# Normalization factors kept as rows in DRAM and applied at the output projection of a hybrid decoder trunk

## The chip, the cores and the metric

The kernel runs on one core of one Trainium2 chip. The metric is the device time of one execution in microseconds. Before the change it is 3005.91 us (median of three runs, 3005.88 to 3008.18). A difference of 0.2% is about 6 us.

## The reference, cut to what matters

A trunk of two layers on a sequence of 1024 tokens and a model width of 1024. Each layer has three head groups that read one normed input, an output projection over their concatenated outputs, and a gated MLP with a convolution. What the change touches is how the three groups are normed before the projection:

```
# recurrent group, width 512, in four blocks of 128
y = gelu(gb) * h
return rmsnorm(y, norm_g)                          # one factor per token over all 512
# differential attention, 4 heads of 128
o = rmsnorm(o, norm_g) * (1.0 - lambda_init)       # one factor per token and head
# mLSTM, 4 heads of 128
h = num / max(|den|, exp(-m))                      # then rmsnorm per token and head,
                                                   # times sigmoid(o_pre)
x = x + concat([recurrent, attention, mlstm]) @ w_out    # 1536 -> 1024
```

So there are nine token factors in a layer: one for the recurrent group, four for the attention heads, four for the mLSTM heads. Each is a vector of 1024 numbers, one per token.

## The kernel before, in words

Activations lie transposed: 128 features on the partitions, 1024 tokens along the free axis, so a block of a head's output is one tile of 128x1024 floats (512 KB). A factor per token is therefore a row that has to stand on all 128 partitions. Matrix products are made of three passes in a rounded format: a high and a low part of both operands, high by high, low by high and high by low (L135 to L137); the parts come from `split`, a cast on ACT (L127) and a subtraction on DVE (L128).

A layer is a mixer (about 0 to 796 us and 1512 to 2296 us) and an MLP (the rest). The mixer's program is a list of steps, ORDER, one list per layer: `R0` to `R3` are the four recurrent blocks, `A0` to `A7` the attention heads in two halves each, `z0` to `z11` the mLSTM's input projections with their convolutions, `M0` to `M7` the mLSTM heads in halves, `y0` to `y2` the loading of four blocks each for the output projection (`y0` recurrent, `y1` attention, `y2` mLSTM) and `w0` to `w5` the projection itself. The steps have priorities in that order, and a scheduler merges them into one fixed instruction list per engine before the program runs. An engine works through its list in order. SP's list is almost only DMA issues, and it too stands still at an issue whose data are not ready.

How a factor comes about: the squares of a block (ACT) are summed over the partitions by `compact`, eight matmuls of one column each, which give a 128x8 tile (token i\*128+p in row p, column i). The inverse root is taken on that small tile on DVE (`rsqrt`, last line L232). Then `bcast_half` turns a half of it into a row on all partitions: four matmuls of 128x128 against an identity into a PSUM bank named `pbc` (L240). DVE multiplies the block with the bank in the same instruction as with the norm's weight (L696 for attention, L891 for the mLSTM), SP stores the block to DRAM (`yd`), and `yload` (L1009) loads it at the projection. For the recurrent group each block's squares have a `compact` of their own (L246, `aux<-ones_d,rg`) and are added up in a small tile, `rgacc`; the row is copied from `pbc` to SBUF by ACT (L996) and multiplied in on DVE at the load (L1011).

SBUF tiles come from pools with few buffers. The pool `mu` has two: the convolution results of the steps `z` live in it until their store to DRAM (`mqk<-mu`, L781) has landed. `yst`, the tile that `yload` loads into, is one of four buffers that it shares with other tiles. Weights come through three buffers, `wraw` (L111), ahead of their use.

Of the kernel before, what the change touches and what calls it, by code (L numbers as in the profile page):

```python
# [17 lines left out]
P = 128  # L18
# [11 lines left out]
D_IN = 2 * RG_W + 3 * DA_W + 4 * ML_W + 8  # L30
D_MIX = 1536
ORDER = (
    "v0 r s0 R0 q0 g q2 q3 q1 A0 z3 z1 v1 A1 z0 A2 R1 z2 A3 A4 A5 M0 M1 z6 A6 A7 z5 z4 z11 M2 z8 R2 M3 R3 z7 z9 z10 y1 M4 y0 M5 w3 M6 s1 w1 M7 w0 w2 y2 w5 w4".split(),
    "R0 q0 q1 g z0 v0 z7 v1 q3 A0 q2 A1 A2 z2 A3 A4 z1 z3 z5 A5 M0 z4 z6 M1 R1 A6 A7 M2 z8 R2 M3 R3 z11 M4 z9 z10 y1 M5 y0 M6 M7 w3 w2 w0 w1 y2 w4 w5".split(),
)
PRI = 4000
FFN_CHUNKS = (8, 6, 8)
# [15 lines left out]
class Trunk:  # L53
# [181 lines left out]
    def bcast_half(self, r, j, ps):  # L235
        nc = self.nc
        pb = ps.tile([P, HALF], F32, tag="aux", name=self.nm("pbc"))
        for i in range(4):
            c = 4 * j + i
            nc.tensor.matmul(pb[:, i * P : (i + 1) * P], r[:, c : c + 1].broadcast_to([P, P]),  # L240
                             self.ident, start=True, stop=True)
        return pb

    def compact(self, pc, sq, ones):
        for i in range(8):
# [221 lines left out]
    def rg(self, l, n):  # L467
        nc, a, d = self.nc, self.a, self.lay[l]
        if n == 0:
            self.rgacc = self.sm("rgacc", (P, 8), bufs=1)  # L470
        for _ in (0,):
            A = self.x16("rg")
            u, r, i, w = (A[:, j, :] for j in range(4))
            self.conv4(l, n * P, d["rcw"], d["rcb"], n, 4, u)
            uh, ul = self.mu("uh", F32R), self.mu("ul", F32R)
            self.split(u, uh, ul)
            self.zfeat(l, RG_W + n * P, lambda z, t: nc.vector.tensor_tensor(w[:, t], z, self.rstd[:, t], ALU.mult))
            nc.scalar.activation(w, w, AF.Gelu_apprx_tanh)
            gh, gl = (self.tp.tile([P, HALF], F32R, tag="qk", bufs=10, name=self.nm("rgw")) for _ in range(2))
            raw = self.tp.tile([P, HALF], F32, tag="st", bufs=2, name=self.nm("rgst"))  # L480
            nc.sync.dma_start(raw[:, :P], a["rg_wa"][l, n])
            nc.sync.dma_start(raw[:, P : 2 * P], a["rg_wx"][l, n])
            self.split(raw[:, : 2 * P], gh[:, : 2 * P], gl[:, : 2 * P])
            for gi, bias, o in ((0, d["ba2"], r), (1, d["bx2"], i)):
                z = self.sc.tile([P, S], F32, tag="sc", name=self.nm("rgz"))
                gs = slice(gi * P, gi * P + P)
                for h in range(2):
                    t = slice(h * HALF, (h + 1) * HALF)
                    self.mm3(z[:, t], [((gh[:, gs], gl[:, gs]), (uh[:, t], ul[:, t]))])
                nc.scalar.activation(o, z, AF.Tanh, bias=bias[:, n : n + 1], scale=0.5)  # L490
            t5 = self.p4("rgt")
            nc.scalar.activation(t5, r, AF.Tanh, bias=d["nls4"][:, n : n + 1], scale=d["nls4"][:, n : n + 1])
            nc.scalar.activation(r, r, AF.Exp, bias=d["ls4"][:, n : n + 1], scale=d["ls4"][:, n : n + 1])
            nc.vector.scalar_tensor_tensor(i, i, 1.0, u, ALU.add, ALU.mult)
            nc.scalar.activation(u, r, AF.Square)
            nc.vector.scalar_tensor_tensor(t5, u, 1.0, t5, ALU.add, ALU.mult)
            nc.scalar.activation(t5, t5, AF.Sqrt, scale=0.25)
            nc.vector.tensor_tensor(i, i, t5, ALU.mult)
            nc.vector.tensor_tensor_scan(u, r, i, 0.0, ALU.mult, ALU.add)
            nc.vector.tensor_tensor(u, u, w, ALU.mult)  # L500
            self.yd[n] = self.dr("yd")
            nc.sync.dma_start(self.yd[n], u)
            nc.scalar.activation(i, u, AF.Square)
            pc = self.aux()
            self.compact(pc, i, self.ones_d)
            if n == 0:
                nc.vector.tensor_copy(self.rgacc, pc[:, :8])
            else:
                nc.vector.tensor_tensor(self.rgacc, self.rgacc, pc[:, :8], ALU.add)
        if n < 3:  # L510
            return
        v = self.sm("nv", (P, 8))
        nc.vector.tensor_scalar(v, self.rgacc, 2.0, EPS, ALU.mult, ALU.add)
        self.rg_r = self.sm("rgr", (P, 8), bufs=1)
        self.rsqrt(self.rg_r, v)

    def da_qk(self, l, h):
        nc = self.nc
# [115 lines left out]
    def da_attn(self, l, h, g):  # L634
# [48 lines left out]
            nc.scalar.copy(o[:, g * HALF : (g + 1) * HALF], acc)  # L683
        if g == 0:
            return
        sq = self.o4("sq")
        nc.scalar.activation(sq, o, AF.Square)
        pc = self.aux()
# [2 lines left out]
        nc.vector.scalar_tensor_tensor(v, ss[:, :, 0], EPS, ss[:, :, 0], ALU.mult, ALU.mult)  # L691
        nc.vector.tensor_tensor(v, v, pc[:, :8], ALU.add)
        self.rsqrt(r, v)
        for j in range(2):
            t = slice(j * HALF, (j + 1) * HALF)
            nc.vector.scalar_tensor_tensor(o[:, t], o[:, t], d["dn2"], self.bcast_half(r, j, self.ps), ALU.mult, ALU.mult)  # L696
        self.yd[4 + h] = self.dr("yd")
        nc.sync.dma_start(self.yd[4 + h], o)

    def ml_rows(self, l):  # L700
        nc, a, d = self.nc, self.a, self.lay[l]
# [117 lines left out]
    def ml_head(self, l, h, hf):  # L819
# [66 lines left out]
        th = self.p4("th")  # L886
        nc.sync.dma_start(th, self.mod[h])
        nc.vector.scalar_tensor_tensor(num, th, 1.0, num, ALU.add, ALU.mult)
        for j in range(2):
            t = slice(j * HALF, (j + 1) * HALF)  # L890
            nc.vector.scalar_tensor_tensor(num[:, t], num[:, t], d["mn2"][:, h : h + 1],  # L891
                                           self.bcast_half(r, j, self.ps), ALU.mult, ALU.mult)
        self.yd[8 + h] = self.dr("yd")
        nc.sync.dma_start(self.yd[8 + h], num)

# [16 lines left out]
    def mixer(self, l):  # L912
        nc = self.nc
        with ExitStack() as c:
            self.zp = self.pool(c, "mz", 2, space=PSUM)
            self.sc = self.pool(c, "msc", 2, space=PSUM)
            self.ps = self.pool(c, "maux", 2, space=PSUM)
            self.tp = self.pool(c, "mt", 2)
            self.yd = [None] * 12
            self.pads = [self.tp.tile([P, S + 3], F32, tag=f"mpad{i}", bufs=1, name=self.nm("mpad"))  # L920
                         for i in range(2)]
            self.npad = 0
            for t in self.pads:
                nc.gpsimd.memset(t[:, 0:3], 0.0)
            if l == 0:
                g0 = self.const.tile([P, 8], F32, name="g0")
                self.rows_to_cols([self.a["attn_norm"][0].rearrange("(n p) -> n p", p=P)], g0)
                self.vw0 = [], []

                def early(k, j):  # L930
                    if j == 0:
                        self.v_weight(0, 2 * RG_W + 2 * DA_W, k, *self.vw0, wide=True)

                self.norm_split(g0, self.ps, lambda j: self.o4("nsq")[:, :HALF], True, True, self.load_x, early)
            else:
                for col in self.first_blocks(ORDER[l]):
                    self.pre[l, col] = self.wblock(self.a["w_in"][l][:, col : col + P], KD)

                def nsq(j):
                    return self.wp.tile([P, HALF], F32, tag="wraw", bufs=3, name=self.nm("nsq"))  # L940

                self.norm_split(self.lay[l]["an"], self.ps, nsq, True, True)
            self.qd, self.kd, self.mqd, self.mkd, self.mod = ([None] * 4 for _ in range(5))
            self.da_state, self.ml_state, self.ys = {}, {}, {}
            self.x = [None] * KD
            for step in ORDER[l]:
                self.step(l, step)
# [18 lines left out]
    def step(self, l, step):  # L966
# [17 lines left out]
        elif k == "A":  # L984
            self.da_attn(l, n // 2, n % 2)
        elif k == "z":
            self.ml_z(l, n // 3, n % 3)
        elif k == "M":
            self.ml_head(l, n // 2, n % 2)
        elif k == "R":  # L990
            self.rg(l, n)
        elif k == "y":
            if n == 0:
                rb = self.mu("rgb")
                for j in range(2):
                    self.nc.scalar.copy(rb[:, j * HALF : (j + 1) * HALF], self.bcast_half(self.rg_r, j, self.ps))  # L996
                self.ys[n] = self.yload(range(4), rb, self.lay[l]["rn"])
            else:
                self.ys[n] = self.yload(range(4 * n, 4 * n + 4))
        elif k == "w":  # L1000
            ms = range(4 * (n % 2), 4 * (n % 2) + 4)
            self.w_out(l, 4 * (n // 2), self.ys[n // 2], self.x[ms[0]] is None, ms)

    def yload(self, ks, rb=None, g=None):
        nc = self.nc
        ys = []
        for k in ks:
            st = self.p4("yst")
            nc.sync.dma_start(st, self.yd[k])  # L1009
            if g is not None:  # L1010
                nc.vector.scalar_tensor_tensor(st, st, g[:, k : k + 1], rb, ALU.mult, ALU.mult)  # L1011
            hi, lo = self.h4("yh"), self.h4("yl")
            self.split(st, hi, lo)
            ys.append((hi, lo))
# [303 lines left out]
```

## Time and profile before

| what | us |
|---|---|
| median of three runs | 3005.91 |
| the profiled execution | 3010.19 |
| its span, first to last instruction | 3008.3 |
| mean granted clock of TensorE in it | 0.975 |
| PE busy | 2902.7 |
| DVE busy | 2066.0 |
| ACT busy | 1347.5 |

The profiled execution is one run under a profiler; durations of single instructions come from it. PE is the matrix engine, PEld its weight loads (beside PE), DVE the vector engine, ACT the scalar engine, POOL GpSimd, SP the engine that issues most DMAs. A timeline row gives start, duration, engine, line, operation and tiles; a number in brackets at its end is how long the engine stood idle before it and what it waited for.

### The profile page before, as it was taken

What the parts mean: (1) busy time and instruction counts of PE and PEld (TensorE: products, weight loads), DVE (VectorE), ACT (ScalarE), POOL (GpSimd) and SP (SyncE); (2) the same over time, 40 slices, a digit from 0 to 9 for tenths busy, and PEclk for the clock granted to TensorE, in tenths of its full rate; (3) what the DMA queues carried; (4) which work ended last, traced back from release to release, by engine and by line L of the source; (5) the groups of instructions that cost most, each with busy time, mean ns of one, the idle gap of its engine ahead of it and who ended that gap; (6) DMA issues with size and microseconds to landing.
All of it is one profiled execution on the core that took longest, in us unless ns stands there. A gap on an engine that the chain in (4) does not pass through costs nothing.

```text
span 3008.3 us, 37082 instructions
## 1 busy us (share of the span) xinstructions
PE 2902.7 (96%) x13433; PEld 2367.9 (79%) x13433; DVE 2066.0 (69%) x3399; ACT 1347.5 (45%) x2160; POOL 281.0 (9%) x304
## 2 busy tenths in 40 slices
PE   8999999999999999999999999999997999999998
PEld 6777777877878888788877877778775888887887
DVE  5674787786688888743484388776756888887434
ACT  4424665653454444422242256565425544444223
POOL 1000001212111111000010000201111111110000
PEclk9999999999999999999999999998998999999999
DMA  5232224454445555542423322324533455556323
GB/s 188 84 98 95 79 68 126 120 172 119 132 97 124 126 126 126 170 146 87 140 74 98 109 74 92 111 75 154 157 104 106 115 123 126 126 126 211 103 70 111
DMA packets 403427, 352.55 MB, mean 117 GB/s; under 512 B 22226, under 2 KB 348684, under 8 KB 403244
## 3 DMA queue, kind: packets, MB, share of 16 engines
q1 hardware_dynamic: 355900, 326.33, 35.1%
q0 software_dynamic: 46464, 23.07, 6.3%
q8 instruction: 105, 1.72, 0.2%
q10 hardware_dynamic: 880, 0.79, 0.1%
q14 instruction: 78, 0.64, 0.1%
HBM read 263.61 MB, written 86.51 MB: 116 GB/s over the span
## 4 chain that ended last, share of the span: by engine, by line
PE 78%; DVE 9%; DMA 5%; ACT 3%; issue 3%; POOL 1%; SPq 0%; DVEq 0%; POOLq 0%; ACTq 0%
PE z L136 22%; PE z L137 22%; PE z L135 22%; DMA R<-Rd 2%; PE aux L246 1%; DMA fst<-fa 1%; PE pbc L240 1%; PE sc L655 1%; PE aux L135 1%; PE sc L656 1%; PE aux L671 1%; PE aux L136 1%; PE aux L137 1%; DVE wlo L128 1%; POOL ds L864 0%
## 5 line engine op out<-in xcount | busy, mean ns | idle before, releaser
L127 ACT CAST whi<-wraw 128x512 fp32r<-128x512 f32 (+1 forms) x420 | 256.8, 613 | 722.3 <-PE z L136 532.9
L128 DVE TENSOR_TENSOR wlo<-wraw,whi 128x512 fp32r<-128x512 f32 (+1 forms) x420 | 286.8, 684 | 156.8 <-ACT whi L127 152.1
L136 PE MATMUL z<-hl,whi 128*128 128x512 f32 x896 | 360.4, 402 | 3.7 <-DVE hl L265 3.6
L135 PE MATMUL z<-hh,whi 128*128 128x512 f32 x896 | 360.6, 403 | 0.9 <-DVE mpad L459 0.9
L137 PE MATMUL z<-hh,wlo 128*128 128x512 f32 x896 | 359.8, 402 | 0.0
L135 PE MATMUL z<-xh,whi 128*128 128x512 f32 x704 | 279.0, 396 | 9.8 <-ACT xh L127 6.5
L136 PE MATMUL z<-xh,whi 128*128 128x512 f32 x704 | 278.5, 396 | 4.4 <-DVE xh L128 4.3
L135 PE MATMUL z<-ah,whi 128*128 128x512 f32 x704 | 273.1, 394 | 5.9 <-ACT ah L127 5.4
L137 PE MATMUL z<-xh,wlo 128*128 128x512 f32 x704 | 276.7, 393 | 0.0
L136 PE MATMUL z<-ah,whi 128*128 128x512 f32 x704 | 274.7, 392 | 0.2 <-DVE ah L128 0.2
L137 PE MATMUL z<-ah,wlo 128*128 128x512 f32 x704 | 274.4, 391 | 0.0
L1148 DVE SCALAR_TENSOR_TENSOR fc<-cv,fpar,fc 128x1024 f32<-128x1024 f32 x176 | 222.1, 1282 | 3.0 <-ACT fc L1145 0.6
L127 ACT CAST whi<-fraw 128x512 fp32r<-128x512 f32 x176 | 108.9, 619 | 241.5 <-PE z L136 237.6
L135 PE MATMUL z<-xu,whi 128*128 128x512 f32 x528 | 205.7, 389 | 0.0
L136 PE MATMUL z<-xu,whi 128*128 128x512 f32 x528 | 205.5, 389 | 0.0
L137 PE MATMUL z<-xu,wlo 128*128 128x512 f32 x528 | 205.1, 389 | 0.0
L136 PEld LDWEIGHTS z<-hl,whi 128*128 128x128 f32 x896 | 171.0, 191 | 39.8 <-DVE hl L265 8.1
L135 PEld LDWEIGHTS z<-hh,whi 128*128 128x128 f32 x896 | 171.4, 191 | 33.3 <-DVE mpad L459 0.9
L137 PEld LDWEIGHTS z<-hh,wlo 128*128 128x128 f32 x896 | 171.3, 191 | 31.2
L1140 POOL DMA_DIRECT2D fraw<-in_w_up_dram x88 | 113.3, 1308 | 771.8 <-DVE cv L1174 395.3
L135 PEld LDWEIGHTS z<-xh,whi 128*128 128x128 f32 x704 | 133.9, 190 | 42.3 <-ACT xh L127 9.8
L135 PEld LDWEIGHTS z<-ah,whi 128*128 128x128 f32 x704 | 132.7, 189 | 37.4 <-ACT ah L127 8.8
(382 smaller groups left out, 6143.9 us busy)
## 6 DMA issues: line engine op xcount, KB each, us to landing
wraw<-in_w_up_dram SPq DMA_DIRECT2D x132, 256.0 KB
wraw<-in_w_in_dram SPq DMA_DIRECT2D x112, 256.0 KB
wraw<-in_w_down_dram SPq DMA_DIRECT2D x112, 256.0 KB
fraw<-in_w_up_dram SPq DMA_DIRECT2D x88, 256.0 KB
fraw<-in_w_up_dram POOLq DMA_DIRECT2D x88, 256.0 KB, 5.7
fa<-fc SPq DMA_DIRECT2D x44, 512.0 KB
xd<-x SPq DMA_DIRECT2D x32, 512.0 KB
x<-xd SPq DMA_DIRECT2D x32, 512.0 KB
```

What stands on the lines that cost most here:

```text
L127: self.nc.scalar.copy(hi, src)
L128: self.nc.vector.tensor_tensor(lo, src, hi.bitcast(F32), ALU.subtract)
L135: nc.tensor.matmul(out, ah, bh, start=start and i == 0, stop=False, **kw)
L136: nc.tensor.matmul(out, ah, bl, start=False, stop=False, **kw)
L137: nc.tensor.matmul(out, al, bh, start=False, stop=stop and i == last, **kw)
L240: nc.tensor.matmul(pb[:, i * P : (i + 1) * P], r[:, c : c + 1].broadcast_to([P, P]), self.ident, start=True, stop=True)
L246: self.nc.tensor.matmul(pc[:, i : i + 1], sq[:, i * P : (i + 1) * P], ones, start=True, stop=True)
L655: nc.tensor.matmul(dst, qq[c][:, qs], k[:, :kn], start=True, stop=False)
L656: nc.tensor.matmul(dst, ql[c][:, qs], k[:, :kn], start=False, stop=kb < g)
L671: nc.tensor.transpose(pa[:, k * P : (k + 1) * P], pp[0][:, (4 * kb + k) * P : (4 * kb + k + 1) * P], self.ident)
L1140: nc.gpsimd.dma_start(t, rows(*more), accum_op=ALU.add)
L1148: nc.vector.scalar_tensor_tensor(o, u[:, j : j + S], cw[:, j, col : col + 1], o, ALU.mult, ALU.add)
```

## The change

Three things are rewritten.

The attention heads, and the mLSTM heads 0 to 2, no longer multiply by their factor before they are stored. The attention head is stored raw, ahead of its squares; the mLSTM head after its gate. The 128x8 tile of factors is written to DRAM by `row_out`, transposed on the way, so that it lies there as one row of 1024 floats. `yload` loads that row onto all 128 partitions (`row_in`, from one row of 4 KB to a tile `yrb` of 512 KB, in the pool `mu`) and DVE multiplies block, weight and row there. Head 3 of the mLSTM is left as it was.

The recurrent group's row goes the same way, in place of `bcast_half` and its copies.

The recurrent squares are no longer reduced block by block. POOL issues a DMA of the 128x1024 tile of squares to DRAM, the first one plain, the other three accumulating in DRAM. A new step, `c`, loads the sum, does one `compact`, takes the inverse root and writes the row. In ORDER it stands behind `z9` in layer 0 and behind `M4` in layer 1.

```
+    def row_out(self, r):
+        t = self.dr("rbd", (8, P))
+        self.nc.sync.dma_start(t.rearrange("i p -> p i"), r)
+        return t
+    def row_in(self, t, dst):
+        self.nc.sync.dma_start(dst, t.rearrange("i p -> (i p)").unsqueeze(0).broadcast_to([P, S]))
+        return dst
 def rg(self, l, n):
...
             nc.scalar.activation(i, u, AF.Square)
-            pc = self.aux()
-            self.compact(pc, i, self.ones_d)
-            if n == 0:
-                nc.vector.tensor_copy(self.rgacc, pc[:, :8])
-            else:
-                nc.vector.tensor_tensor(self.rgacc, self.rgacc, pc[:, :8], ALU.add)
...
+            nc.gpsimd.dma_start(self.rgacc, i, **({"accum_op": ALU.add} if n else {}))
+    def rg_stats(self):
+        t5 = self.p4("rgs")
+        nc.sync.dma_start(t5, self.rgacc)
+        pc = self.aux()
+        self.compact(pc, t5, self.ones_d)
+        v, r = self.sm("nv", (P, 8)), self.sm("nr", (P, 8))
+        nc.vector.tensor_scalar(v, pc[:, :8], 2.0, EPS, ALU.mult, ALU.add)
+        self.rsqrt(r, v)
+        self.rg_r = self.row_out(r)
 def da_attn(self, l, h, g):
+        self.yd[4 + h] = self.dr("yd")
+        nc.sync.dma_start(self.yd[4 + h], o)
...
-        for j in range(2):
-            t = slice(j * HALF, (j + 1) * HALF)
-            nc.vector.scalar_tensor_tensor(o[:, t], o[:, t], d["dn2"], self.bcast_half(r, j, self.ps), ALU.mult, ALU.mult)
-        self.yd[4 + h] = self.dr("yd")
-        nc.sync.dma_start(self.yd[4 + h], o)
+        self.yrow[4 + h] = self.row_out(r), d["dn2"]
 def ml_head(self, l, h, hf):
-        for j in range(2):
...
+        if h < 3:
+            self.yrow[8 + h] = self.row_out(r), d["mn2"][:, h : h + 1]
+        else:
+            for j in range(2):
...
 def yload(self, ks, rb=None, g=None):
+            elif k in self.yrow:
+                row, w = self.yrow[k]
+                nc.vector.scalar_tensor_tensor(st, st, w, self.row_in(row, self.mu("yrb")), ALU.mult, ALU.mult)
```

What the scheduler makes of it is seen at three places of layer 0. The first is SP's list where step `y1` prepares the output projection, between the last recurrent block and the loads of the following mLSTM half. `mqk<-mu` are the stores of the steps `z7`, `z9` and `z10`, `wraw` are weights, `st` and `E` the next mLSTM half's data. Before:

```order
248 L597 DMA st_5636<-mqk_5456 128x512
249 L597 DMA st_5642<-vd_2098 128x4x128
250 L111 DMA wraw_6355<-in_w_out_dram 128x4x128
251 L781 DMA mqk_5529<-mu_5458 128x1024
252 L111 DMA wraw_6389<-in_w_out_dram 128x4x128
253 L111 DMA wraw_6423<-in_w_out_dram 128x4x128
254 L781 DMA mqk_5602<-mu_5531 128x1024
255 L597 DMA st_5806<-mqk_4034 128x512
```

After the change (`rbd<-nr` is the recurrent row's way out, `yrb<-rbd` the attention rows' way in; the load of the summed squares, `rgs`, stands six rows above this piece):

```order
250 L788 DMA mqk_5417<-mu_5346 128x1024
251 L246 DMA rbd_5446<-nr_5431 128x8x1
252 L606 DMA st_5565<-mqk_5344 128x512
253 L606 DMA st_5571<-vd_2089 128x4x128
254 L250 DMA yrb_5523<-rbd_2538 128x1024
255 L111 DMA wraw_6229<-in_w_out_dram 128x4x128
256 L111 DMA wraw_6263<-in_w_out_dram 128x4x128
257 L111 DMA wraw_6297<-in_w_out_dram 128x4x128
258 L914 DMA x_6531<-xd_325 128x1024
259 L914 DMA x_6531<-xd_332 128x1024
260 L788 DMA mqk_5519<-mu_5448 128x1024
261 L250 DMA yrb_5532<-rbd_3235 128x1024
```

The attention rows stand behind the stores of the convolution tiles, whose buffers they share: the first behind the store of `z9`, the second behind the store of `z10`, the third and fourth two and five rows further on, at rows 263 and 266. Before, no load of the projection's left operand stood there; the attention blocks had been loaded earlier.

The second place is PE's list where the last input projection `z10` (tiles `hh`, `hl`) ends and the output projection (`yh`, `yl`) begins. Before:

```order
2543 L136 MATMUL z_5570<-hl_118,whi_5540 128x512
2544 L137 MATMUL z_5570<-hh_117,wlo_5541 128x512
2545 L135 MATMUL z_5974<-yh_5606,whi_5968 128x512
2546 L136 MATMUL z_5974<-yl_5607,whi_5968 128x512
2547 L137 MATMUL z_5974<-yh_5606,wlo_5969 128x512
2548 L135 MATMUL z_5974<-yh_5612,whi_5968 128x512
```

After the change, at the same place:

```order
2530 L136 MATMUL z_5487<-hl_118,whi_5457 128x512
2531 L137 MATMUL z_5487<-hh_117,wlo_5458 128x512
2532 L135 MATMUL ms_5585<-qh_5561,kh_5567 128x512
2533 L136 MATMUL ms_5585<-ql_5562,kh_5567 128x512
2534 L135 MATMUL ms_5603<-qh_5561,kh_5567 128x384
2535 L136 MATMUL ms_5603<-ql_5562,kh_5567 128x384
2536 L137 MATMUL ms_5585<-qh_5561,kl_5568 128x512
2537 L137 MATMUL ms_5603<-qh_5561,kl_5568 128x384
2538 L135 MATMUL z_5882<-yh_5526,whi_5876 128x512
2539 L135 MATMUL z_5896<-yh_5526,whi_5876 128x512
2540 L136 MATMUL z_5882<-yl_5527,whi_5876 128x512
```

And 20 rows further on, where the second and third attention block (`yh_5535`, `yh_5544`) come in:

```order
2559 L136 MATMUL aux_5577<-W_5626,vh_5573 128x256
2560 L137 MATMUL aux_5577<-W_5626,vl_5574 128x256
2561 L135 MATMUL z_5882<-yh_5535,whi_5876 128x512
2562 L135 MATMUL z_5896<-yh_5535,whi_5876 128x512
2563 L136 MATMUL z_5882<-yl_5536,whi_5876 128x512
2564 L137 MATMUL z_5882<-yh_5535,wlo_5877 128x512
2565 L135 MATMUL z_5882<-yh_5544,whi_5876 128x512
```

Products of the mLSTM half `M4` (`ms`, `aux<-W`) are now between `z10` and the projection, and between its blocks; the fourth block comes in at row 2597. The third place is PE's list at the sums of the recurrent squares of the last block. Before, with the block's own tile, with 66 rows between it and the block's last product:

```order
2489 L137 MATMUL z_5497<-hh_113,wlo_5468 128x512
2490 L135 MATMUL z_5497<-hh_115,whi_5467 128x512
2491 L246 MATMUL aux_5359<-ones_d,rg_5185 128x1 x8
2492 L136 MATMUL z_5497<-hl_116,whi_5467 128x512
2493 L137 MATMUL z_5497<-hh_115,wlo_5468 128x512
```

After, with the tile loaded back from DRAM, with 110 rows between:

```order
2495 L135 MATMUL z_5461<-hh_111,whi_5457 128x512
2496 L136 MATMUL z_5461<-hl_112,whi_5457 128x512
2497 L255 MATMUL aux_5421<-ones_d,rgs_5419 128x1 x8
2498 L137 MATMUL z_5461<-hh_111,wlo_5458 128x512
2499 L135 MATMUL z_5461<-hh_113,whi_5457 128x512
```

The three other `compact` rows of the recurrent blocks are gone from the layer, and so are the `pbc` rows of seven heads and of the recurrent group.

## Rows read from the trace of the kernel before

**Rows 1.** The page's shares of engines: busy time, share of the span, instructions.
```profile
PE 2902.7 (96%) x13433; PEld 2367.9 (79%) x13433; DVE 2066.0 (69%) x3399; ACT 1347.5 (45%) x2160; POOL 281.0 (9%) x304
```
**Rows 2.** Windows, the two mixers: length, busy PE, PEld, DVE, ACT, POOL, clock, DMA share, GB/s.
```profile
0.00:796.00 796.00, 756.45 (x3662) 613.80 (x3663) 546.83 (x1070) 374.83 (x639) 83.97 (x108) 0.96 0.38 114
...
1512.00:2296.00 784.00, 756.34 (x3683) 615.22 (x3682) 524.57 (x956) 360.08 (x609) 78.20 (x97) 0.97 0.36 108
```
**Rows 3.** The page's chain that ended last, by engine.
```profile
PE 78%; DVE 9%; DMA 5%; ACT 3%; issue 3%; POOL 1%; SPq 0%; DVEq 0%; POOLq 0%; ACTq 0%
```
**Rows 4.** Tile pbc: durations in ns (min/median/max), first and last start.
```profile
L240 PE MATMUL pbc<-identr,nr x320: 271/275/580, 41.2 to 2327.0; 128*128 128x128 f32 x160
...
L240 PE MATMUL pbc<-identr,rgr x32: 270/346/421, 660.5 to 2161.1; 128*128 128x128 f32 x32
...
L696 DVE SCALAR_TENSOR_TENSOR o<-o,par,pbc x16: 732/746/750, 329.7 to 2016.8; 128x512 f32<-128x512 f32 x16
```
**Rows 5.** PE's timeline at one attention head's two halves.
```profile
328.61 1.95 PE L240 MATMUL pbc<-identr,nr 128*128 128x128 f32 x16
330.39 0.22 PE L657 MATMUL sc<-cmaskb,identb 128*128 128x128 bf16 x1
```
**Rows 6.** PE's timeline at the first recurrent block's sums.
```profile
129.39 1.95 PE L246 MATMUL aux<-ones_d,rg 128*128 128x1 f32 x16 [0.49 <-ACT rg L503]
131.20 0.48 PE L136 MATMUL z<-hl,whi 128*128 128x512 f32 x1
```
**Rows 7.** PE's waits: total us, times, longest us.
```profile
PE aux L246 <- ACT rg L503: 10.4, 7, 3.2
...
PE pbc L240 <- DVE nr L232: 1.9, 2, 1.6
...
PE z L136 <- DVE yl L128: 1.8, 2, 1.1
```
**Rows 8.** PE's timeline behind the third recurrent block's sums in layer 1.
```profile
2051.11 3.57 PE L246 MATMUL aux<-ones_d,rg 128*128 128x1 f32 x16 [3.17 <-ACT rg L503]
...
2063.32 0.63 PE L136 MATMUL z<-hl,whi 128*128 128x512 f32 x1
2063.75 0.55 PE L137 MATMUL z<-hh,wlo 128*128 128x512 f32 x1
```
**Rows 9.** Windows, two stretches of layer 1 behind recurrent sums; columns as in rows 2.
```profile
2050.00:2062.00 12.00, 10.89 (x41) 10.17 (x42) 6.04 (x9) 3.03 (x7) 2.36 (x3) 0.52 0.46 150
2090.00:2098.00 8.00, 7.59 (x32) 7.11 (x33) 4.18 (x16) 0.76 (x2) 0.29 (x1) 0.59 0.47 140
```
**Rows 10.** SP's timeline, layer 0: stores of z9 and z10, a load of 256 KB.
```profile
634.80 0.33 SPq L781 DMA_DIRECT2D mqk<-mu  x1
...
644.61 0.34 SPq L781 DMA_DIRECT2D mqk<-mu  x1
...
652.43 0.37 SPq L837 DMA_DIRECT2D E<-Rd  x1
```
**Rows 11.** ACT's timeline, the first use of that load.
```profile
656.16 0.72 ACT L838 ACTIVATE E<-E,mle 128x512 f32<-128x512 f32 x1 [1.09 <-DMA E<-Rd]
```
**Rows 12.** PE's timeline, layer 0, from the input to the output projection.
```profile
632.53 0.39 PE L137 MATMUL z<-hh,wlo 128*128 128x512 f32 x1
632.75 0.39 PE L135 MATMUL z<-yh,whi 128*128 128x512 f32 x1
...
638.17 0.50 PE L136 MATMUL z<-yl,whi 128*128 128x512 f32 x1 [1.15 <-DVE yl L128]
```
**Rows 13.** Line L1011: durations in ns, first and last start.
```profile
L1011 DVE SCALAR_TENSOR_TENSOR yst<-yst,par,rgb x8: 1273/1280/1284, 665.2 to 2171.3; 128x1024 f32<-128x1024 f32 x8
```
**Rows 14.** The page's DMA issues: KB each, median us to landing.
```profile
fraw<-in_w_up_dram POOLq DMA_DIRECT2D x88, 256.0 KB, 5.7
```
**Rows 15.** Tile scr: a load of 1024 pieces of 32 bytes, and its first use.
```profile
L704 SPq DMA_DIRECT2D scr<-in_w_in_dram x2: 368/397/426, 123.6 to 1579.8; - x2
L127 ACT CAST gp<-scr x2: 227/232/238, 129.2 to 1584.6; 128x64 fp32r<-128x64 f32 x2
```
**Rows 16.** SP's own waits for weight buffers: total us, times, longest us.
```profile
SPq L111 <- DVE wlo L128: 717.3, 214, 16.2
```

More of the change, by code (lines that the diff above doesn't have):

```diff
@@ L32 @@
 ORDER = (
-    "v0 r s0 R0 q0 g q2 q3 q1 A0 z3 z1 v1 A1 z0 A2 R1 z2 A3 A4 A5 M0 M1 z6 A6 A7 z5 z4 z11 M2 z8 R2 M3 R3 z7 z9 z10 y1 M4 y0 M5 w3 M6 s1 w1 M7 w0 w2 y2 w5 w4".split(),
-    "R0 q0 q1 g z0 v0 z7 v1 q3 A0 q2 A1 A2 z2 A3 A4 z1 z3 z5 A5 M0 z4 z6 M1 R1 A6 A7 M2 z8 R2 M3 R3 z11 M4 z9 z10 y1 M5 y0 M6 M7 w3 w2 w0 w1 y2 w4 w5".split(),
+    "v0 r s0 R0 q0 g q2 q3 q1 A0 z3 z1 v1 A1 z0 A2 R1 z2 A3 A4 A5 M0 M1 z6 A6 A7 z5 z4 z11 M2 z8 R2 M3 R3 z7 z9 c z10 y1 M4 y0 M5 w3 M6 s1 w1 M7 w0 w2 y2 w5 w4".split(),
+    "R0 q0 q1 g z0 v0 z7 v1 q3 A0 q2 A1 A2 z2 A3 A4 z1 z3 z5 A5 M0 z4 z6 M1 R1 A6 A7 M2 z8 R2 M3 R3 z11 M4 c z9 z10 y1 M5 y0 M6 M7 w3 w2 w0 w1 y2 w4 w5".split(),
 )
@@ L469, in rg @@
         if n == 0:
-            self.rgacc = self.sm("rgacc", (P, 8), bufs=1)
+            self.rgacc = self.dr("rgacc")
         for _ in (0,):
@@ L503, in rg @@
             nc.scalar.activation(i, u, AF.Square)
-            pc = self.aux()
-            self.compact(pc, i, self.ones_d)
-            if n == 0:
-                nc.vector.tensor_copy(self.rgacc, pc[:, :8])
-            else:
-                nc.vector.tensor_tensor(self.rgacc, self.rgacc, pc[:, :8], ALU.add)
[L510 to L515, printed above, removed]
+            nc.gpsimd.dma_start(self.rgacc, i, **({"accum_op": ALU.add} if n else {}))
+    def rg_stats(self):
+        nc = self.nc
+        t5 = self.p4("rgs")
[6 more added lines that the diff above has]
+        self.rg_r = self.row_out(r)
     def da_qk(self, l, h):
@@ L888, in ml_head @@
         nc.vector.scalar_tensor_tensor(num, th, 1.0, num, ALU.add, ALU.mult)
-        for j in range(2):
-            t = slice(j * HALF, (j + 1) * HALF)
-            nc.vector.scalar_tensor_tensor(num[:, t], num[:, t], d["mn2"][:, h : h + 1],
-                                           self.bcast_half(r, j, self.ps), ALU.mult, ALU.mult)
+        if h < 3:
+            self.yrow[8 + h] = self.row_out(r), d["mn2"][:, h : h + 1]
+        else:
+            for j in range(2):
+                t = slice(j * HALF, (j + 1) * HALF)
+                nc.vector.scalar_tensor_tensor(num[:, t], num[:, t], d["mn2"][:, h : h + 1],
+                                               self.bcast_half(r, j, self.ps), ALU.mult, ALU.mult)
         self.yd[8 + h] = self.dr("yd")
@@ L918, in mixer @@
             self.tp = self.pool(c, "mt", 2)
-            self.yd = [None] * 12
+            self.yd, self.yrow = [None] * 12, {}
             self.pads = [self.tp.tile([P, S + 3], F32, tag=f"mpad{i}", bufs=1, name=self.nm("mpad"))
@@ L993, in step @@
             if n == 0:
-                rb = self.mu("rgb")
-                for j in range(2):
-                    self.nc.scalar.copy(rb[:, j * HALF : (j + 1) * HALF], self.bcast_half(self.rg_r, j, self.ps))
+                rb = self.row_in(self.rg_r, self.mu("rgb"))
                 self.ys[n] = self.yload(range(4), rb, self.lay[l]["rn"])
@@ L999, in step @@
                 self.ys[n] = self.yload(range(4 * n, 4 * n + 4))
+        elif k == "c":
+            self.rg_stats()
         elif k == "w":
```

## The prediction

> **What bounds the kernel now.** I began with the page's shares of engines: PE is busy for 2902.7 of 3008.3 us, DVE for 2066.0 [rows 1]. The chain of waits says the same, 78% of it on PE and 9% on DVE [rows 3]. So what leaves PE's list is worth nearly its issue time, and what makes PE wait costs its length. The windows by stage came next, since only the two mixers change: PE is busy there for 756 us of 796 and of 784, so a mixer has 40 and 28 us of idle PE, and a mean clock of 0.96 and 0.97 [rows 2]. That idle time and that clock are what the change can win back beside its matmuls, and what it can enlarge. Then I looked at the tiles that disappear (`pbc`, the recurrent sums), at PE's waits, and at the place where the projection begins.
>
> **The factor rows on PE.** A half is four fp32 matmuls, which the trace counts as eight instructions; it has 352 of them in all [rows 4]. Seven heads and one recurrent row leave in each layer, that is 16 pairs of halves, 16 x 16 = 256 instructions. A pair holds PE from 328.61 to 330.39, 1.8 us [rows 5], and PE runs straight on behind it: no gap took it up. 16 x 1.8 = 28.8 us less.
>
> **The recurrent sums on PE.** Eight `compact` calls become two. One takes PE from 129.39 to 131.20, 1.8 us [rows 6]; 6 x 1.8 = 10.8 us less. PE also waited 10.4 us in seven of the eight for ACT's squares [rows 7]; I take 6 of it as gone, between 0 (if the next instruction in PE's list waits for something of the same chain) and 10.4. Of the small waits of `pbc` for `rsqrt`, 1.9 us [rows 7], I take all, rounded to 2.
>
> **The clock behind these places.** After the wait of 3.17 us for the squares in layer 1, the sums at 2051.11 and what follows run on matmuls of 0.63 us, until 2063.75 [rows 8]; the granted clock there was 0.52, and 0.59 behind the next sums [rows 9], the lower of the two levels. A 128x512 matmul begins every 0.43 us there [rows 8] against 0.22 us elsewhere [rows 12]. Over these 20 us about half the pace was lost, some 9 us, but part of the slow stretch belongs to other narrow products of the mLSTM half that stay. With the smaller ones of layer 0, I take 8 us as regained; the ends are 0 (the stretch starts anyway, from the narrow products that stay) and 16.
>
> Gains in all: 28.8 + 10.8 + 6 + 2 + 8 = 55.6 us.
>
> **Applying the rows at the projection.** Fourteen heads swap two DVE instructions of 0.746 us [rows 4] for one of about 1.28 us, by the recurrent one that has the same form [rows 13]: DVE's total falls a little, 20.9 less 17.9 us, which is nothing where DVE is not the bound. But the work moves to where the projection starts. There PE goes from the last product of `z10` at 632.53 to the first of the projection at 632.75 and waits 1.15 us once on `yl` [rows 12], 1.8 us in all [rows 7]. The attention blocks are ready because nothing but a load and a split stands ahead of them. With the change each needs its row first, and the rows come through the two `mu` buffers that `z9` and `z10` hold until their stores have landed. Those stores go out at 634.80 and 644.61 [rows 10], which is 2.3 and 12.1 us behind `z10`'s last product. What waits is SP: in its list behind the first row stand three weight loads and the store of `z10`, behind the later rows the loads of the next mLSTM half, and they wait with it.
>
> How late the blocks get: a load of 256 KB issued at 652.43 was used at 656.16, 3.7 us [rows 10, 11]; a store or a row of 512 KB I take at 4 to 5 us. The store of `z9` has landed at +7, the first row at +11.5, multiplication and split take 1.3 + about 2.3: first block at about +15. The second row goes out behind the store of `z10`, at +12.5, the third when that store has landed, the fourth when the second product has freed its buffer: the last block at about +24. PE has 10 to 11 us of other work there, the mLSTM's products that now stand between (six `ms`, then the `aux<-W`) and the parts of the projection that need only earlier blocks. The stall is so about 13 us, less the 2 to 4 us that PE already loses there: 9 us per layer, 18 in all. Bounds: 5 (the scheduler's fill is as good as it looks) and 35 (17 a layer, with nothing to fill). For the recurrent row and for the mLSTM's rows I take nothing: they are issued a projection step earlier than their use, and the product of `w0` to `w3` hides them; without that cover each would be a row's 5 us.
>
> **The recurrent sum through DRAM.** Now the squares of the last block are ready about 15 us behind its last product (66 matmuls at the 0.22 us of [rows 12], and a wait like the 0.5 us of [rows 6]). Then follow an issue on POOL and the accumulation (256 KB issued by POOL landed after 5.7 us [rows 14]; 512 KB that also reads its target I bound by 5.7 and 10), and a load (3.7 us as above, up to 5 for 512 KB): 24.5 to 30 us. PE's list has 110 matmuls ahead of the sum in layer 0, 24 us, and 129 in layer 1, 28 us. So PE waits about 3 us in layer 0 and 1 in layer 1; a wait of that size is followed by a slow stretch as in [rows 8], for which I add 3 us: 7 in all, between 0 and 20. The SP list stands at `rgs` for the same time, with the last two stores behind it; this is in the projection's bounds.
>
> The Trainium skill, in "DMA: Bandwidth & Descriptors", section on the anatomy of a DMA issued by GpSimd, fits such a transfer as 2.0 us plus its bytes over 436 KB per us; for 512 KB that would be an estimate of 3.2 us, under the 5.7 us that this trace has for half the bytes [rows 14]. By that rule PE would not wait for the sum at all, and the total would be 7 us lower.
>
> **The writes of the rows.** Sixteen of them, each of 1024 single floats. The nearest row is a load of 1024 pieces of 32 bytes: issued at 123.6, used at 129.2, 5.6 us [rows 15], 1.9 us more than the plain load above. Nothing waits for a write before the projection, many us later; what can wait are transfers behind it in the same queues. SP waited 717.3 us for weight buffers to come free, 214 times, 3.4 us each on the mean [rows 16]: weights are loaded as far ahead as their buffers allow, and a delay of some us meets that lead. I take 3 us in all for the writes and the shuffled lists, between -10 and +20; the rival below takes the far end.
>
> Costs: 18 + 7 + 3 = 28 us. The sum is 55.6 - 28 = 27.6 us less. The profiled execution took 3010.19 us around a span of 3008.3, so it would be about 2982.6; the median of the runs is 4.3 us below the profiled one, and the forecast is 2978 us.
>
> **Rivals.** *The projection's start is filled after all.* The mLSTM's products between the blocks cover the rows, the sum's wait is nil and more of the clock returns: 55.6 us of gains with some 0 to 3 of costs, 2951 us. For it: a scheduler placed the products there. Against: it did so by its own durations, and the row loads hang on the stores, which follow the products by 12 us whatever it thought [rows 10]. Chance 0.20.
>
> *The waits replace the matmuls.* The transitions cost 15 us a layer and the sums 7 each, clock included, and the clock is not regained behind the narrow products: 47.6 of gains against 30 + 14 + 3 of costs, which is about 3005 us. For it: PE is in order, and the first projection product stands eight rows behind `z10` with no long work ahead of it. Against: 40 us of pure issue time are gone for good. Chance 0.11, within 0.2%.
>
> *The single floats clog the queues.* Each `row_out` keeps the DMA queues busy with 1024 tiny writes, and the weight loads behind it come late; PE waits at the following product. It decides from 27.6 / 16 = 1.7 us of PE time per write. For 5 us each it is 80 us: 2978 + 80 = 3058 us. For it: no row shows writes this small, and every write stands between weights in SP's list. Against: the load of 1024 pieces took only 1.9 us more than a plain one, and the weights' lead of 3.4 us on the mean covers that. Chance 0.16, all of it slower.
>
> The Trainium skill speaks for this one, on the same page: its specifications say that transfers under 512 bytes cost a read-modify-write, and its rules for kernel authors that a last dimension that is not contiguous becomes one descriptor per element. It gives no time for such a write, and no row here shows one.
>
> **How the numbers follow.** The forecast's own case has 0.53; its terms' bounds put it between 2955 and 2999 us. Faster by more than 0.2% (6 us, about what a measurement of this kernel can tell from no change) is that case and the first rival, 0.73. Within 0.2% is the second rival, 0.11. Slower is the third, 0.16. The range for 8 in 10 goes from 2946 to 3012: it leaves out most of the slow rival and the rim of the fast one.
>
> **What would show it.** In the changed profile PE's `pbc` should count 96 instructions, its busy time in the mixers should fall by about 20 us each, and the wait of PE for the last recurrent squares should appear once per layer, on the load `rgs`, at 1 to 4 us. At the end of `z10` PE should stand about 13 us in pieces, released by `yh` or `yl`, with DVE behind it released by the DMA of `yrb`. Waits of PE on `whi` or `wlo` behind each `rbd<-nr` would show the third rival. The forecast fails if the start of the projection costs over 20 us a layer, or if weights come late.

## The result and the profile after

The changed kernel takes 3120.78 us (median of four runs, 3115.36 to 3124.58) against 3006.56 us for the kernel before: 1.0376 times as long, 95% interval 1.0361 to 1.0392, or 114 us slower. 2978 us were forecast. The profiled execution took 3115.36 us, its span 3113.7 us, at a mean granted clock of 0.958.

The page's shares of engines answer to [rows 1]:

```profile
PE 2898.9 (93%) x13081; PEld 2340.2 (75%) x13081; DVE 2059.0 (66%) x3377; ACT 1347.0 (43%) x2156; POOL 287.7 (9%) x312
```

PE is busy as long as before and the span is 105 us longer: the time went into PE standing still. The chain that ended last says on what, beside [rows 3]:

```profile
PE 74%; DMA 10%; DVE 9%; issue 3%; ACT 3%; POOL 1%; SPq 0%; DVEq 0%; POOLq 0%; ACTq 0%
```

DMA went from 5% to 10%. At the head of PE's waits (total us, times, longest us) stand groups that were small before or not there, and the longest of [rows 7] is gone:

```profile
PE aux L135 <- ACT W L127: 21.3, 5, 10.7
PE sc L664 <- ACT p L670: 21.0, 10, 8.4
PE ms L135 <- ACT kh L127: 20.2, 3, 14.4
PE aux L135 <- ACT pT L127: 18.2, 3, 10.3
PE ms L135 <- DVE R L863: 13.6, 2, 12.5
```

Three of the five stood in the list before, much shorter:

```profile
PE aux L135 <- ACT W L127: 5.9, 3, 3.4
PE ms L135 <- DVE R L856: 2.3, 1, 2.3
PE sc L655 <- ACT p L661: 1.5, 2, 1.3
```

These are operands of the attention and the mLSTM, not weights and not the rows. In time the longest wait of each group stands behind a `row_out`. SP's timeline at the first one:

```profile
325.85 0.37 SPq L246 DMA_DIRECT2D rbd<-nr  x1
327.99 0.38 SPq L111 DMA_DIRECT2D wraw<-in_w_in_dram  x1
329.18 0.36 SPq L606 DMA_DIRECT2D st<-vd  x1
```

ACT's and PE's timelines of the same stretch, where that `st` is used:

```profile
340.93 0.62 ACT L127 CAST vh<-st 128x512 fp32r<-128x512 f32 x1 [8.86 <-DMA st<-vd]
```

```profile
342.08 0.80 PE L135 MATMUL aux<-pT,vh 128*128 128x512 f32 x1 [7.37 <-ACT pT L127]
```

A load issued at 329.18 is used at 340.93, 11.8 us, where [rows 10, 11] had 3.7 us for the same 256 KB. Windows over it (columns as in [rows 2]) show what the DMA engines did meanwhile:

```profile
325.80:327.80 2.00, 2.00 (x12) 1.51 (x11) 1.68 (x4) 1.98 (x6) 0.00 (x0) 1.00 0.25 6
327.80:337.80 10.00, 6.17 (x29) 4.55 (x27) 6.23 (x11) 2.37 (x4) 0.00 (x0) 1.00 0.50 16
337.80:340.80 3.00, 0.00 (x0) 0.00 (x0) 0.00 (x0) 0.00 (x0) 0.00 (x0) 0.74 0.92 237
```

For ten us the engines are half busy and move 16 GB/s, with four loads issued; then 237 GB/s. The `row_out` holds them, and everything issued behind it stands until about 12 us after its issue. The same picture follows nearly every one of the 16 writes. PE ends a wait of 4 to 14 us some 12 to 23 us behind 12 of them; this is the longest, behind the write of the recurrent row at 664.34, at the start of the projection:

```profile
679.38 0.80 PE L135 MATMUL ms<-qh,kh 128*128 128x512 f32 x1 [14.38 <-ACT kh L127]
```

### The profile page after: what moved, and what is told of

Same layout as the page of the kernel before. It is cut to its first block, busy times and chain, and to the rows that moved or that the text cites. A ratio compares the mean times of both kernels' runs of the same rounds, so it can differ in the third digit from the quotient of the medians.

```text
span 3113.7 us, 36423 instructions
## 1 busy us (share of the span) xinstructions
PE 2898.9 (93%) x13081; PEld 2340.2 (75%) x13081; DVE 2059.0 (66%) x3377; ACT 1347.0 (43%) x2156; POOL 287.7 (9%) x312
## 4 chain that ended last, share of the span: by engine, by line
PE 74%; DMA 10%; DVE 9%; issue 3%; ACT 3%; POOL 1%; SPq 0%; DVEq 0%; POOLq 0%; ACTq 0%
PE z L136 21%; PE z L137 21%; PE z L135 21%; DMA R<-Rd 3%; DMA fst<-fa 1%; DMA st<-vd 1%; DMA st<-mqk 1%; PE aux L255 1%; PE sc L664 1%; PE sc L665 1%; DVE wlo L128 1%; PE aux L680 1%; PE aux L135 1%; DMA wraw<-in_w_out_dram 1%; PE aux L137 1%
## 5 line engine op out<-in xcount | busy, mean ns | idle before, releaser
L135 PE MATMUL z<-yh,whi 128*128 128x512 f32 x384 | 155.7, 408 | 11.9 <-ACT yh L127 11.5
```

What stands on the lines that cost most here:

```text
L135: nc.tensor.matmul(out, ah, bh, start=start and i == 0, stop=False, **kw)
```

## The experiments

All ratios are against the kernel before on the same chip, with a 95% interval.

**Row turned on PE (e1).** The 128x8 tile is transposed by one matmul, copied into a free part of the square's tile, and written as eight rows of 512 bytes.

```
     def row_out(self, r, sq):
         t = self.dr("rbd", (8, P))
-        self.nc.sync.dma_start(t.rearrange("i p -> p i"), r)
+        pt = self.aux()
+        self.nc.tensor.transpose(pt[:8, :P], r, self.ident)
+        rt = sq[:8, :P]
+        self.nc.vector.tensor_copy(rt, pt[:8, :P])
+        self.nc.sync.dma_start(t, rt)
```

> The changed kernel, with the factor tile turned on PE (one matmul of 128 columns against the identity, one DVE copy) so that each row goes out as 8 pieces of 512 bytes instead of 1024 pieces of 4. Theory A (a write of 1024 single floats holds the DMA queues for about 11 us, and the loads behind it come late): about 2980 us, 2965 to 3000, with no PE waits of 5 us or more behind the row writes. Theory B (the row loads and the new order of the loads before the projection cost the time): 3100 us or more, as the row loads and the order stay.

3009.03 us, 1.0014 (1.0003 to 1.0026), above theory A's 2965 to 3000 and far from theory B. The writes of single floats are some 110 of the 114 us. But the 28 us of gain did not come either, so a second loss was left to find.

**Row written as it lies (e2).**

```
-        self.nc.sync.dma_start(t.rearrange("i p -> p i"), r)
+        self.nc.sync.dma_start(t.rearrange("i p -> (i p)").rearrange("(q j) -> q j", j=8), r)
```

> The changed kernel, with the factor tile written as it lies, 128 pieces of 32 bytes, no work on PE or DVE added. The row that comes back has its tokens in another order, so the factors go to the wrong tokens; all else is as in the changed kernel. Theory A, by the count of pieces: an eighth of the hold, about 1.4 us, so 2975 to 2995 us. If instead any write of small pieces costs the same, 3110 us. Theory B: 3110 us.

3003.93 us, 1.0001 (0.9982 to 1.0021). 128 pieces of 32 bytes hold nothing up; three us behind the first write the loads run:

```profile
329.40:332.40 3.00, 3.00 (x15) 2.46 (x14) 2.88 (x7) 1.63 (x2) 0.00 (x0) 1.00 0.65 173
```

The time is again some 20 us above what theory A gave for it.

**Writes from ACT's queue (e3).** `self.nc.scalar.dma_start` in place of `self.nc.sync.dma_start` in `row_out`.

> The changed kernel, with the writes of single floats issued from ACT's queue and not from SP's; pieces as they were. If SP's queue alone is held (later transfers of the same queue stand behind the pieces): 2975 to 3000 us. If the DMA engines themselves are held, whatever queue the pieces come from: 3090 to 3130 us. Theory B: about 3120 us.

3106.51 us, 1.0340 (1.0319 to 1.0362). It is not the order in SP's queue: written from ACT's queue the row holds SP's loads almost as long. The stretch behind the first write:

```profile
327.90:336.90 9.00, 6.14 (x29) 4.51 (x27) 6.18 (x11) 2.32 (x4) 0.00 (x0) 1.00 0.50 16
```

**The writes alone (e4).** The kernel before with `self.row_out(r)` added at the places where the change has it, nothing read back.

> The kernel before, with the 16 writes of single floats added at the places where the changed kernel has them and nothing else; nobody reads them. Theory A: 16 writes at 6 to 8 us of PE time each, 3100 to 3130 us. Theory B: 3005 to 3015 us, since no row is loaded and the loads keep their order.

3087.90 us, 1.0278 (1.0252 to 1.0305): 83 us for 16 writes that nobody reads, 5.2 us each, less than the 6 to 8 of theory A. In the changed kernel the same writes cost more, 110 us. The waits that are longer there lie in layer 1: behind the writes of the attention heads 29.5 us (they end at 1875.73, 1939.09 and 1994.82) against 3 here, and at the start of the projection 19 against 3. What makes the same writes cost more there was not tried.

**Shifted back by 64 bytes (e5).** In the trace of the changed kernel, of e1 and e2 one more thing stood out: the MLP, which the change does not touch, ran fewer matmuls per 100 us at a granted clock of 1.00. Windows over 100 us of it, before, after, in that order:

```profile
1050.00:1150.00 100.00, 100.00 (x443) 82.84 (x442) 83.89 (x106) 47.87 (x71) 12.85 (x10) 1.00 0.53 121
```

```profile
1050.00:1150.00 100.00, 100.00 (x437) 81.64 (x436) 82.71 (x105) 46.55 (x69) 12.71 (x10) 1.00 0.53 121
```

The groups of instructions narrow it to products whose moving operand is `xu`; first before, then after (busy us, mean ns):

```profile
L135 PE MATMUL z<-xu,whi 128*128 128x512 f32 x528 | 205.7, 389 | 0.0
L136 PE MATMUL z<-xu,whi 128*128 128x512 f32 x528 | 205.5, 389 | 0.0
```

```profile
L135 PE MATMUL z<-xu,whi 128*128 128x512 f32 x528 | 208.2, 394 | 0.0
L136 PE MATMUL z<-xu,whi 128*128 128x512 f32 x528 | 208.1, 394 | 0.0
```

In the timelines they follow each other every 0.2333 us against 0.2267 us. `xu` lies in a pool of the MLP behind the pool of small tiles, and there the change had dropped `rgacc` and `rgr`, 32 bytes each per partition: by the tiles' addresses in the program, `xu` begins 32 bytes past a multiple of 128 instead of 96.

```
+        self.sm("pad", (P, 16), bufs=1)
         self.pre = {}
```

> The run with turned rows (e1), with an unused tile of 64 bytes per partition added to the pool of small tiles. The changed kernel has lost two tiles of 32 bytes there (the recurrent sums and factors), so every tile of the pools behind lies 64 bytes lower than before; this puts them back. Theory C (the place of the moving operand sets the pace of its matmuls: the MLP's products on xu, and on the ah tiles of the same pool, went from 0.2267 to 0.2333 us per matmul, 1584 + 576 of them): 14 us less than e1, and 0.2267 us on xu again. Rival D (the pace comes from something else in the changed kernel, its DMAs or its longer lists): as e1 within 3 us.

2993.03 us, 0.9960 (0.9946 to 0.9974): 15 us less than e1 against before, by 64 unused bytes. In the traces the two MLPs, from the first product on `xh` or `xu` to the last on `ah`, take 1378 us before, 1393 in e1 and 1378 here. The group again reads:

```profile
L136 PE MATMUL z<-xu,whi 128*128 128x512 f32 x528 | 205.9, 390 | 0.0
```

**The kernel before, shifted (e6).** The same line in the kernel before.

> The kernel before, with an unused tile of 64 bytes per partition in the pool of small tiles and nothing else; its instructions stand in the same order on every engine. Theory C: the MLP's xu and ah tiles now lie 64 bytes off, at the same remainder of 128 bytes as in the changed kernel, 0.2333 us per matmul on them, about 14 us slower than before less 1 to 3 us gained in the mixer: ratio 1.004. Rival D: ratio 1.000.

3015.08 us, 1.0026 (1.0009 to 1.0044), 8 us slower by the ratio and 11 by the medians, with every instruction in the same order. The three passes on `xu` are not slowed alike here:

```profile
L136 PE MATMUL z<-xu,whi 128*128 128x512 f32 x528 | 208.3, 394 | 0.0
L138 PE MATMUL z<-xu,wlo 128*128 128x512 f32 x528 | 206.8, 392 | 0.0
L137 PE MATMUL z<-xu,whi 128*128 128x512 f32 x528 | 205.3, 389 | 0.0
```

So theory C holds as to the place, not as to the rule in it: the remainder of 128 bytes is the same as in the changed kernel, and the slowdown about half (on `xu` 4.1 us of busy time more than before, in the changed kernel 7.8). What exactly of the place counts stays open.

**Attention as before (e7).** From e5, `da_attn` is set back.

```
-        self.yrow[4 + h] = self.row_out(r, sq), d["dn2"]
+        for j in range(2):
+            t = slice(j * HALF, (j + 1) * HALF)
+            nc.vector.scalar_tensor_tensor(o[:, t], o[:, t], d["dn2"], self.bcast_half(r, j, self.ps), ALU.mult, ALU.mult)
+        self.yd[4 + h] = self.dr("yd")
+        nc.sync.dma_start(self.yd[4 + h], o)
```

> The run e5 with the attention heads as in the kernel before (factor spread on PE, block multiplied before its store); mLSTM heads 0 to 2 and the recurrent group with turned rows through DRAM. Theory T (the attention rows hang on the stores of z9 and z10 and hold PE at the start of the projection, 17 us of waits in e1 and a slow stretch behind them, against 8 pairs x 1.8 = 14.4 us of matmuls saved): about 10 us faster than e5. Rival (those waits were only moved from elsewhere): 14 us slower than e5, the matmuls that come back.

2976.36 us, 0.9900 (0.9869 to 0.9931): 17 us faster than e5, though the 14.4 us of matmuls came back. The start of the projection in layer 0, PE's timeline of e5:

```profile
625.70 1.22 PE L136 MATMUL z<-yh,whi 128*128 128x512 f32 x2 [6.07 <-ACT yh L128]
...
631.34 1.22 PE L136 MATMUL z<-yh,whi 128*128 128x512 f32 x2 [1.99 <-ACT yh L128]
```

The 60 us around it, in e5 and then in e7 (busy PE, PEld, DVE, ACT, POOL, clock, DMA share, GB/s):

```profile
600.00:660.00 60.00, 43.26 (x162) 33.76 (x162) 42.56 (x60) 20.54 (x30) 10.47 (x8) 0.74 0.66 208
```

```profile
600.00:660.00 60.00, 53.02 (x239) 41.73 (x239) 46.87 (x70) 28.12 (x40) 8.09 (x9) 0.94 0.73 232
```

With the attention rows PE is idle for 17 of these us and the granted clock is 0.74; without them 7 us and 0.94. By an estimate from these two rows, 43.26 us of work at 0.74 lose 11 us to the clock and 53.02 us at 0.94 lose 3, so the clock costs here about as much as the waits do.

**Recurrent part as before (e8).** From e1, `rg`, `y0` and ORDER are those of the kernel before, so that the two small tiles are back and nothing is shifted.

> The run e5 with the recurrent group as in the kernel before (a sum per block on PE, the factor spread on PE); attention heads and mLSTM heads 0 to 2 with turned rows through DRAM. By the terms of the prediction the recurrent part is worth 6 x 1.8 + 2 x 1.8 us of matmuls and 6 to 10 us of waits, less some 8 for the wait on the summed squares: so 12 to 16 us slower than e5. If the sum through DRAM gives its gain back (its wait of 4 us and the slow clock behind it): equal to e5 within 4 us.

2996.09 us, 0.9973 (0.9959 to 0.9986), 3 us slower than e5, with intervals that overlap, and so the second case of the expectation. The recurrent sum through DRAM is worth next to nothing beside the attention rows. What it is worth without them was not tried.

**Other shifts (e9, e10), from e7.** e9 adds `self.const.tile([P, 8], F32, name="padc")` as the first tile, e10 adds `self.tp.tile([P, 16], F32, tag="padm", bufs=1, name=self.nm("padm"))` at the head of the mixer's pool.

> The run e7, with an unused tile of 32 bytes per partition in the first pool, so that every tile of SBUF lies 32 bytes higher: the moving operands of the projections and of the MLP now start on multiples of 128 bytes (before: 96 over), those of the mixer's pool 64 over (before: 32 over). If the pace only knows 32 over as slow: 0 to 5 us faster than e7, from the mixer's pool. If a start on a multiple of 128 is faster still than 96 over, as 96 is faster than 32 by 0.0066 us: up to 13400 x 0.0066 = 60 us faster, 0.220 us per matmul. If the start is slower there: more than e7.

> The run e7, with an unused tile of 64 bytes at the head of the mixer's pool, so that the moving operands in it go from 32 to 96 over a multiple of 128, and nothing else moves. Theory C: some 1000 wide products with a moving operand from that pool (v, attention, mLSTM) gain up to 0.0066 us each: 2 to 6 us faster than e7. Rival: equal to e7.

2975.22 us, 0.9888 (0.9862 to 0.9914), and 2979.92 us, 0.9915 (0.9883 to 0.9948). Neither can be told from e7. A start on a multiple of 128 is not faster than 96 bytes past it.

The trace of e10 also speaks against the remainder of 128 as the rule. The v projection's moving operand `vwh` lies in the mixer's pool: 32 bytes past a multiple of 128 before, 96 past in the changed kernel, and 96 past in e10, there 128 bytes higher. Its products before, after and in e10 (ns, min/median/max):

```profile
L135 PE MATMUL z<-vwh,hh x240: 388/394/776, 13.6 to 1710.3; 128*128 128x512 f32 x120
```

```profile
L135 PE MATMUL z<-vwh,hh x240: 387/389/775, 13.4 to 1766.3; 128*128 128x512 f32 x120
```

```profile
L136 PE MATMUL z<-vwh,hh x240: 387/393/775, 13.0 to 1696.7; 128*128 128x512 f32 x120
```

With the same remainder the median is 389 ns in one kernel and 393 in the other, about the 394 of the other remainder. The place counts, but not by its remainder of 128 alone.

**What sets the hold (e11 to e14).** All are e4 with another `row_out`. e11 writes half the columns:

```
-        self.nc.sync.dma_start(t.rearrange("i p -> p i"), r)
+        self.nc.sync.dma_start(t[:4].rearrange("i p -> p i"), r[:, :4])
```

> The run e4 (the kernel before with the 16 unread writes) with half of each write, 512 single floats instead of 1024. If the hold goes by the count of pieces: about half of e4's 83 us or less, since part of each hold is covered by the weights' lead: 3025 to 3045 us. If a write of single floats costs the same whatever its count: 3085 us.

3077.92 us, 1.0224 (1.0192 to 1.0255). Half the pieces, 71 of the 83 us: the count is not it. e12 writes one column (`t[:1]`, `r[:, :1]`).

> The run e4 (the kernel before with the 16 unread writes) with one column of the factor tile alone: 128 single floats, all into one row of 512 bytes. Halving the pieces left the hold at 11 us, so a count over all pieces is out. Theory R (writes of single floats into one row of 512 bytes go one after another, rows beside each other): the hold of 11 us stays, 128 floats still meet in the row, 3075 to 3090 us. If the hold goes with the count below 512 pieces after all: 3005 to 3020 us.

3063.11 us, 1.0187 (1.0116 to 1.0258). 128 single floats still cost 59 us, less than theory R's 3075 to 3090 but far from no hold. The next two keep all 1024 and change where they land:

```
 # e13: a partition's eight floats in 64 bytes of their own
+        t = self.dr("rbd", (P, 16))
+        self.nc.sync.dma_start(t[:, 0:16:2], r)
 # e14: in the turned order, each 512 bytes from the next
+        t = self.dr("rbd", (8 * P, P)).rearrange("(i p) c -> p i c", p=P)
+        self.nc.sync.dma_start(t[:, :, 0], r)
```

> The run e4 with 1024 single floats as before, but not turned: the eight floats of a partition go side by side (8 bytes apart) into 64 bytes of their own. As many pieces, of the same size, from the same tile; only where they land differs. Theory R: hardly any two DMA engines meet in a place, 3005 to 3030 us. If single floats are slow wherever they go: 3085 us.

> The run e4 with 1024 single floats in the turned order, each 512 bytes from the next in DRAM, so that no two lie in the same 512 bytes. Theory R: no hold, 3005 to 3030 us. If single floats are slow wherever they go, or the turned order of the source is what is slow: 3085 us.

3034.64 us, 1.0100 (1.0074 to 1.0126), a little above theory R's 3005 to 3030, and 3002.84 us, 0.9994 (0.9972 to 1.0015). The hold behind the first write in e12, e13 and e14, each with the stretch that follows it:

```profile
333.50:341.50 8.00, 7.93 (x42) 6.34 (x41) 3.32 (x6) 1.07 (x4) 0.00 (x0) 1.00 0.48 38
341.50:344.50 3.00, 0.00 (x0) 0.00 (x0) 0.96 (x3) 2.17 (x6) 0.00 (x0) 1.00 0.71 252
```

```profile
333.90:339.90 6.00, 6.00 (x35) 5.08 (x34) 3.36 (x6) 1.11 (x4) 0.00 (x0) 1.00 0.32 32
339.90:342.90 3.00, 1.99 (x9) 1.31 (x7) 0.42 (x1) 1.45 (x4) 0.00 (x0) 1.00 0.80 288
```

```profile
329.00:331.00 2.00, 1.92 (x14) 1.70 (x14) 1.74 (x5) 1.90 (x5) 0.00 (x0) 1.00 0.23 2
331.00:334.00 3.00, 3.00 (x22) 2.61 (x21) 2.97 (x6) 1.05 (x4) 0.00 (x0) 1.00 0.76 216
```

Eight us at 38 GB/s for 128 floats in one row of 512 bytes, six us at 32 GB/s where 64 floats share 512 bytes, and none for 1024 floats that lie 512 bytes apart: two us behind the issue the loads run at 216 GB/s. What is left of theory R is this: many floats that land close together hold the loads, whatever their whole count. The length goes with how many share 512 bytes: eight us for 128 of them, six for 64, and for the 16 pieces of 32 bytes that share one in e2 none is to be seen. How the 512 bytes come in is not shown: stretches of 256 or 1024 were not tried, and e14 also spreads the floats over 512 KB of DRAM where e4 has 4 KB.

## Why the prediction was wrong, point by point

**The step that failed** is the last one of the costs: "I take 3 us in all for the writes and the shuffled lists, between -10 and +20". It was 110 us in the changed kernel (from 1.0376 to 1.0014 in e1) and 83 us alone (e4). The bound came from [rows 15], a load of 1024 pieces of 32 bytes, read for its count of pieces. The count was the wrong thing to read, as e11 and e14 show, and a load into as many places says nothing of writes into one. The third rival had the mechanism, writes that keep the queues busy, and nearly its price (5 us a write against 5.2 to 7), at a chance of 0.16. What was held up were not the weights with their lead of [rows 16] but operands loaded a few us before use, which have none. The Trainium skill's rule on pieces under 512 bytes ("DMA: Bandwidth & Descriptors", Specifications) spoke against the change and was right in direction; e14, with pieces as small, shows that the size alone cost nothing here.

**A term that was missing**: 64 bytes of SBUF. The sum left the MLP out as untouched. It became some 15 us slower by where its tiles came to lie (e1 against e5): 0.0066 us on the 1584 products on `xu` and 576 on `ah`, 14 us by the timelines.

**The matmuls that go** went: `pbc` counts 96 instructions, as foretold. PE's busy time did not fall by 20 us a mixer: the mean granted clock is 0.958 in place of 0.975, and at the lower level the same matmuls are busy longer. In e2, where the writes hold nothing up and the clock is 0.977, the page's busy time is 2876.4 us, 26 less than before, although its MLP is slowed as in e1. The 2 us for small waits of `pbc` were misread: the same row stands in the list of the changed kernel, 1.9 us in two waits, as these waits belong to the norms ahead of mixer and MLP.

**The start of the projection** was seen in the right place and priced too low. With the writes mended, e5 shows 9.6 us of waits on `yh` and `yl` in layer 0 and 9.4 in layer 1, but e7 puts the whole at 17 + 14.4 = 31 us, some 15 us a layer against the 9 taken, near the upper bound of 35 in all. Much of the difference is the clock: over windows of 5 us in e5 it is 0.50 from 625 to 635 and again from 645 to 650, in e7 1.00. The term for a regained clock, 8 us, left this loss out; whether the clock came back elsewhere is not shown.

**The recurrent sum** waited as foretold, on the load of the sum:

```profile
650.88 3.54 PE L255 MATMUL aux<-ones_d,rgs 128*128 128x1 f32 x16 [3.65 <-DMA rgs<-rgacc]
```

3.65 us in layer 0; layer 1 had none that the waits list. The eight DMAs of squares landed after 4.4 to 8.5 us, median 7.0; two are plain (4.4 and 4.6), and the last of each layer, which the sum waits for, took 5.2 and 7.9, against bounds of 5.7 to 10. By the fit of the Trainium skill ("DMA: Bandwidth & Descriptors", the section on the anatomy of a DMA issued by GpSimd) the estimate was 3.2 us and no wait; the measurement decides for the rows. Its gain was nonetheless about 3 us (e8), where the terms gave 13: saved products and waits were given back.

**The other terms** came near: without the writes and the shift, e5 is 11 us faster than before, against 31 by the sum without the 3 us. The projection's 13 us and the recurrent part's 10 about fill that gap. So of the 143 us between forecast and result some 107 are the writes, 15 the shifted tiles and 20 the projection and the sum. The range was narrow, too: added up, the terms' own bounds reach from about 2933 to 3039 us, not from 2955 to 2999.

The version that beats both kernels is e7, with e9 and e10 beside it: mLSTM rows turned on PE, the recurrent part through DRAM, the attention as before, 1.0% faster than before. Why it gains 28 us, more than the sum of its parts in e5 and e8 explains, stays open.

## What to carry to other kernels

Do not transpose a small tile by a DMA that scatters single floats into shared rows of DRAM: turn it on PE and write whole rows. Here a write of 4 KB stalled loads of 256 KB for 10 us. When a stage that was not edited changes its pace at full clock, compare where its tiles lie before looking for a cause in the schedule, and put back what was dropped with an unused tile. Price a row that is needed at a change of stage with the buffers it waits for and with the clock after the wait.

## What the runs showed of the hardware

Two things were not expected. 128 floats of 4 bytes into one row of 512 bytes hold SP's loads for 8 us at 38 GB/s (e12), and 1024 into eight rows for 9 to 10 us at 16 GB/s, from SP's queue (the changed kernel) and from ACT's (e3) alike; 1024 floats 512 bytes apart do not (e14, 216 GB/s). And at the same granted clock of 1.00 the products on `xu`, of 128x512 floats, follow each other every 0.2267 us where the kernel before has its tiles, and every 0.2333 us 64 bytes lower; 64 bytes higher (e6) one pass of the three is as slow in busy time (208.3 us), one between (206.8) and one not slowed (205.3). Which property of the address decides stays open.
